# Prompt attention output through DRAM, layer norms placed between output-projection products, and lower step rates

## The chip, the core and the metric

The kernel runs on one core of a Trainium2 chip. The core has a matrix engine (PE in the profile, with PEld for its weight loads), a vector engine (DVE), an activation engine (ACT), a general engine (POOL) and a queue engine (SP) that here issues all DMAs. Each engine works its own instructions in a fixed order, and an instruction that waits holds up all behind it on that engine. On-chip memory is SBUF; matrix products land in eight PSUM banks of 128 x 512 floats. The metric is the device time of one execution in microseconds (us), lower is better.

## What is computed

Two batches, a prompt of 512 rows and a sample of 1024 rows, go through one encoder layer with shared weights (width 1024):

```
h = rmsnorm(x); z = h @ w_in                      # q | k | v | ca | cb
a = windowed attention(q, k, v), blocks of 128 rows, 8 heads, 2 kv groups
c = ca * sigmoid(cb); c = depthwise conv(31)(c); c = silu(layernorm(c))
x = x + concat(a, c) @ w_out
h = rmsnorm(x); u = depthwise conv(3)(h @ w_up)
x = x + (silu(gate) * value) @ w_down
y = rmsnorm(x)
```

All data is float32. A matrix product is done as three products of rounded parts (high x high, high x low, low x high), so every operand is first split in two by ACT (the high part) and POOL or DVE (the low part).

## The kernel before

**Order.** The program is written as one Python stream, and the place of an instruction in that stream is its priority. A planner then sets each engine's order: whenever an engine is free in its model of time, it takes the ready instruction of the best priority. On the chip this order is fixed. Slots in SBUF (`Slots`, 61 of 2 KB named h, 15 of 4 KB named q that can be halved, and a few others) and PSUM banks (a, u, b, c) are handed out in the order of the stream, so a new tile in a used slot waits for the last reader of the old one.

**Stages.** First, 14 column chunks of `w_in` are multiplied with the prompt (`step(i, 0)`). Then the same 14 chunks are loaded again and multiplied with both halves of the sample (28 products, `step(i, 1)` and `step(i, 2)`); beside these runs the prompt's own side work, the generator `prompt()`. Then follow 22 steps of the prompt's feed-forward part (`ffn_step`), beside which the sample's attention runs (`sample()`), then the sample's output projection and its feed-forward part.

**How side work is dosed.** A product of one chunk (`proj`) is 24 matmuls and calls `tick()` four times. A tick adds `pace["rate"]` to an account, and for every full unit one step (up to the next `yield`) of the front generator in `side` is put into the stream. The rates are `RB` beside the 28 products and `RBO` once the prompt's attention is through. What is left of `side` when the products are all in the stream is put behind them by `drain(side)`.

**The long convolution.** Each of 4 channel groups of a batch is a generator (`conv_items`): 27 (prompt) or 24 (sample) taps on DVE per 512 columns, one tap an item, and the other taps on ACT and POOL. `tick()` also gives credit for these items, at `CA` and then `CB` for the prompt's (`convs`), and, once these are through, at `CL`, `CLO` and `CD` in turn for the sample's (`late`). `behind` gives an item a priority that is `BACK` places later than its place in the stream.

**The prompt's side work before.** `attention(0, 8)` runs eight units (4 blocks of 128 rows, two kv groups each): `scores(u)` and `values(u)`. After each of units 4 to 7 one `conv_norm(i)` is run, for blocks 0 to 3; the first begins with `drain(convs)`, which puts all unfinished prompt convolution into the stream at that point. `values` leaves the attention's output of a block in two tiles `cats[i, 0]` (high and low part), and `conv_norm` the convolution's in `cats[i, 1]`. Then, for each half `n` of the output columns, the weights are loaded and split (`load_wo`, `split_wo`), and `out_half(i, n)` does 24 matmuls for each block (L726 to L728). The last half of a block adds the residual (L731), sums squares (L737) and computes the factor of the next norm. `make_h2` scales the four blocks (L776) and turns them (L258, with L260 and L261 taking the result to SBUF), which is the input of the feed-forward part.

**`conv_norm` step by step.** Load the block's convolution output (L684); four transposes into a bank (L690); mean and variance (L692, L693, on DVE); the factor (L176, L177, on POOL); scale (L696, DVE); four transposes back (L702); scale and bias (L705, four on ACT); tanh (L707); product (L708); high and low part (L709 on ACT, L710 on DVE).

The sample's attention output already goes through DRAM: `values` stores it to `catd` and `load_cat` fetches it.

Of the kernel before, what the change touches and what calls it, by code (L numbers as in the profile page):

```python
# [9 lines left out]
F32 = mybir.dt.float32  # L10
# [5 lines left out]
P = 128  # L16
D = 1024
KC = D // P
# [18 lines left out]

RA, RB, RBO, RD, RN, RE = 1.2, 0.8, 2.5, 0.8, 0.95, 0.9  # L40


CA, CB = 0.9, 0.4
CL, CLO, CD = 0.6, 1.0, 0.6

NOFF = (4, 7)

# [3 lines left out]
WOP, WOA, DW, DW2 = 1, 5, 2, 0  # L51
# [5 lines left out]
KEEP = 3  # L57


BACK = (200, 1500)  # L60
U0 = 2


# [82 lines left out]
def tile_hybrid_encoder(ctx: ExitStack, tc: tile.TileContext, xs, rel_bias, norm_attn_g, w_in,  # L146
                        attn_sink, conv_dw_w, conv_dw_b, conv_ln_g, conv_ln_b, w_out, norm_ffn_g,
                        w_up, ffn_dw_w, ffn_dw_b, w_down, norm_final_g, onehot, outs):
    nc = tc.nc
    cst = ctx.enter_context(tc.tile_pool(name="cst", bufs=1))  # L150
    big = ctx.enter_context(tc.tile_pool(name="big", bufs=1))
    dr = ctx.enter_context(tc.tile_pool(name="dr", bufs=1, space=bass.MemoryType.DRAM))
# [156 lines left out]
    qsd = [dr.tile([4, P, NH, P], F32, name=f"qsd{i}") for i in range(3)]  # L309
    vsd = dr.tile([P, 2, NKV, 4, P], F32, name="vsd")  # L310
    ksd = dr.tile([HD, NKV, 2, 1024], F32, name="ksd")
    catd = dr.tile([8, P, 2, 4 * P], F32, name="catd")
    cvd = [dr.tile([P, 4, G["T"]], F32, name=f"cvd{G['g']}") for G in GR]
    rs2 = cst.tile([P, 12], F32, name="rs2")

# [129 lines left out]
    def step(i, nt):  # L445
# [4 lines left out]
        if kind == "ca" and nt != 1:  # L450
            g = 0 if nt == 0 else 1
            (convs, late)[g].append(behind(conv_items(g, c, cpads.pop((g, c))), BACK[g]))
        tick()
# [76 lines left out]
    blocks = [(G, b) for G in GR for b in range(G["nb"])]  # L530
    NB = len(blocks)
    qt, cats, units = {}, {}, {}
# [86 lines left out]
    def values(u):  # L619
        i, kv = divmod(u, 2)  # L620
        G, b = blocks[i]
        kts = window(i)
        cat = cat_of(i, 0)
        pr = units.pop(u)
        nt0 = 0 if i < 4 else 1
        ht = []

        def turn(n):
            pt = bank("attn")
            for j in range(GRP):  # L630
                nc.tensor.transpose(pt[:, j * P:(j + 1) * P], pr[j][:, 1 + n * P:1 + (n + 1) * P], ident[:])
            hi, lo = sb.tile([NT], F32R), sb.tile([NT], F32R)
            nc.scalar.copy(hi[:], pt[:])
            nc.vector.tensor_tensor(lo[:], pt[:], hi[:].bitcast(F32), op=ALU.subtract)
            ht.append((hi, lo))

        turn(0)
        yield 0.0
        turn(1)
        po = bank("attn")  # L640
        for n, k in enumerate(kts):
            yield 0.0
            hi, lo = ht[n]
            v = vt[nt0 + k // 4][kv][:, k % 4, :]
            nc.tensor.matmul(po[:], v, hi[:], start=(n == 0), stop=False)
            nc.tensor.matmul(po[:], v, lo[:], start=False, stop=(n == len(kts) - 1))
            ht[n] = hi = lo = None
            if n + 2 < len(kts):
                turn(n + 2)
        rows = slice(kv * HD, (kv + 1) * HD)  # L650
        rest = slice((1 - kv) * HD, (2 - kv) * HD)
        c, d = sb.tile([NT]), sb.tile([NT])
        nc.scalar.copy(c[rows, :], po[rest, :])
        nc.scalar.copy(cat[0][rows, :, :], po[rows, :].rearrange("p (j t) -> p j t", t=P))
        nc.vector.tensor_tensor(d[rows, :], po[rows, :], cat[0][rows, :, :].bitcast(F32).rearrange("p j t -> p (j t)"),
                                op=ALU.subtract)
        nc.gpsimd.tensor_tensor(cat[1][rows, :, :].rearrange("p j t -> p (j t)"), d[rows, :], c[rows, :], op=ALU.add)
        if kv == 1 and G["g"] == 1:
            cats.pop((i, 0))
            for L in range(2):  # L660
                nc.sync.dma_start(catd[b, :, L, :].rearrange("p (j t) -> p j t", t=P), cat[L][:].bitcast(F32))
        yield 0.0

    def attention(u0, u1, then={}):
        yield from scores(u0)
        for u in range(u0, u1):
            if u + 1 < u1:
                yield from scores(u + 1)
            yield from values(u)
            if u in then:  # L670
                yield from then[u]

    def load_cat(i):
        cats[i, 0] = (sb.tile([4, P], F32R), sb.tile([4, P], F32R))
        for L in range(2):
            nc.sync.dma_start(cats[i, 0][L][:].bitcast(F32), catd[blocks[i][1], :, L, :].rearrange("p (j t) -> p j t", t=P))

    def conv_norm(i):
        G, b = blocks[i]
        if G["g"] == 0:  # L680
            drain(convs)
        cat = cat_of(i, 1)
        cv = sb.tile([4, P])
        nc.sync.dma_start(cv[:], cvd[G["g"]][:, :, b * P:(b + 1) * P])  # L684
        if G["g"] == 1 and (i, 0) not in cats:
            load_cat(i)
        yield 0.0
        pt = bank("norm")
        for c in range(4):
            nc.tensor.transpose(pt[:, c * P:(c + 1) * P], cv[:, c, :], ident[:])  # L690
        st, mv, rs = sm(6), sm(2), sm(1)
        nc.vector.bn_stats(st[:], pt[:])  # L692
        nc.vector.bn_aggr(mv[:], st[:])  # L693
        rstd_of(mv[:, 1:2], 1.0, rs[:])
        xh = sb.tile([CCH])
        nc.vector.tensor_scalar(xh[:], pt[:], mv[:, 0:1], rs[:], op0=ALU.subtract, op1=ALU.mult)  # L696
        del pt
        for _ in range(YN):
            yield 0.0
        p2 = bank("norm")  # L700
        for c in range(4):
            nc.tensor.transpose(p2[:, c * P:(c + 1) * P], xh[:, c * P:(c + 1) * P], ident[:])  # L702
        y, t = sb.tile([4, P]), sb.tile([4, P])
        for c in range(4):
            nc.scalar.activation(y[:, c, :], p2[:, c * P:(c + 1) * P], AF.Identity,  # L705
                                 scale=lng[:, c:c + 1], bias=lnb[:, c:c + 1])
        nc.scalar.activation(t[:], y[:], AF.Tanh)  # L707
        nc.vector.scalar_tensor_tensor(t[:], t[:], 1.0, y[:], op0=ALU.add, op1=ALU.mult)  # L708
        nc.scalar.copy(cat[0][:], t[:])  # L709
        nc.vector.tensor_tensor(cat[1][:], t[:], cat[0][:].bitcast(F32), op=ALU.subtract)  # L710
        yield 0.0

    xr, x1, wo = {}, {}, {}
    x1d = [dr.tile([P, D], F32, name=f"x1d{i}") for i in range(12)]

    def out_half(i, n):
        G, b = blocks[i]
        if i not in xr:
            xr[i] = load_x(G, b)
        x = xr[i]  # L720
        po = bank("out")
        s = slice(n * NT, (n + 1) * NT)
        for kc in range(KC):
            wh, wl = wo[kc, n]
            ch, cl = (t[:, kc % 4, :] for t in cats[i, kc // 4])
            nc.tensor.matmul(po[:], ch, wh[:], start=(kc == 0), stop=False)  # L726
            nc.tensor.matmul(po[:], ch, wl[:], start=False, stop=False)
            nc.tensor.matmul(po[:], cl, wh[:], start=False, stop=(kc == KC - 1))  # L728
            if kc % 2 == 1 and kc < KC - 1:
                yield 0.0  # L730
        nc.vector.tensor_tensor(x[:, s], po[:], x[:, s], op=ALU.add)  # L731
        if n == 1:
            x1[i] = x
            nc.sync.dma_start(x1d[i][:], x[:])
            ss = sm(1)
            junk = sb.tile([D], BF16, 2)
            nc.scalar.activation(junk[:], x[:], AF.Square, accum_out=ss[:])  # L737
            rstd_of(ss[:], D, rs2[:, i:i + 1])
            cats.pop((i, 0)), cats.pop((i, 1))
            xr.pop(i)  # L740
        yield 0.0
# [3 lines left out]
    def load_wo(kc, n):  # L745
        raw = wor[kc, n] = sb.tile([NT])
        s = slice(n * NT, (n + 1) * NT)
        if kc < 4:
            for kv in range(NKV):
                r0 = (kv * GRP + kc) * HD  # L750
                nc.sync.dma_start(raw[kv * HD:(kv + 1) * HD, :], w_out[0, r0:r0 + HD, s])
        else:
            nc.sync.dma_start(raw[:], w_out[0, kc * P:(kc + 1) * P, s])
# [28 lines left out]

    use.update(step="b", turn="a", attn="au", norm="au", out="u")

    def prompt():
        yield from attention(0, 8, {u: conv_norm(u - 4) for u in range(4, 8)})
        kt.clear(), vt.clear(), qt.clear(), bias.clear()
        pace.update(rate=RBO, late=CLO)
        for n in range(2):
            for kc in range(KC):  # L790
                if (kc, n) not in wor:
                    load_wo(kc, n)
            yield 0.0
            for kc in range(KC):
                split_wo(kc, n, kc % 2 < DW)
                if kc % 2 == 1:
                    yield 0.0
            for i in range(4):
                if n == 0 and i == 3:
                    for kc in range(WOP):  # L800
                        load_wo(kc, 1)
                yield from out_half(i, n)
            wo.clear()
        yield from make_h2(0, 0)

    seq = [(GR[0], j) for j in range(NJ)]
# [142 lines left out]
    L, R = slice(0, NT), slice(NT, W2)  # L949
# [634 lines left out]
    u, e, o11, o12 = (acc.pop(n) for n in ("u", "e", "o11", "o12"))  # L1584
# [73 lines left out]
```

## Time and profile before

| | |
|---|---|
| median of 3 runs | 1564.66 us (1561.09 to 1566.85) |
| the profiled execution | 1561.29 us |
| its span, first to last instruction | 1559.5 us |
| mean granted PE clock | 0.99 |
| PE busy | 1505.8 us, 97% of the span |
| DVE busy | 1126.9 us, 72% |
| ACT busy | 795.2 us, 51% |
| POOL busy | 709.7 us, 46% |
| DMA | 227.17 MB, mean 146 GB/s |

Times of places are in us from the first instruction. A row of the windows view gives a stretch, its length, then for each engine the busy time and the number of instructions, then the granted clock of PE (1.00 is full speed), the share of the DMA engines and GB/s. A row of the timeline gives the start, the length, engine, line, operation and, in square brackets, how long the engine had been idle and what ended that wait. `q<-a` is a write to a tile of class q from one of class a.

### The profile page before, as it was taken

How to read it: one execution, taken by the hardware profiler on the slowest of the kernel's cores; microseconds unless marked ns; L12 is line 12 of the kernel's file. 1: busy time of each engine (PE TensorE's matmuls, PEld its weight loads, DVE VectorE, ACT ScalarE, POOL GpSimd, SP SyncE). 2: the span in 40 equal slices, each digit the busy share in tenths (PEclk: the TensorE clock that was granted, in tenths of full speed). 3: DMA queues.
4: the chain of work that ended last, by engine and by line, in shares of the span. 5: the costliest groups of instructions: out<-in, count | busy, mean ns of one | idle time of the engine just before them, and what ended most of it. 6: DMA issues, size and time to landing. Idle time of an engine off the chain costs nothing. (4 is left out here: it accounts for less than half of the span.)

```text
span 1559.5 us, 20112 instructions
## 1 busy us (share of the span) xinstructions
PE 1505.8 (97%) x6843; PEld 1228.9 (79%) x6843; DVE 1126.9 (72%) x1604; ACT 795.2 (51%) x1404; POOL 709.7 (46%) x566
## 2 busy tenths in 40 slices
PE   8998998899999999899999999999999999999997
PEld 6787787787888888777777888888888788888885
DVE  7999767858789785334868777777776845569883
ACT  4634654335787786623455445554545543444354
POOL 6652343226666775947434555555544000003355
PEclk9999999899999999999999999999999999999999
DMA  7582334447344346779332333333332582357644
GB/s 229 157 212 78 108 99 124 128 131 226 111 132 130 117 130 182 241 235 305 108 95 75 102 101 102 102 102 102 102 115 75 191 280 82 105 166 233 220 132 162
DMA packets 228780, 227.17 MB, mean 146 GB/s; under 512 B 13268, under 2 KB 168348, under 8 KB 228549
## 3 DMA queue, kind: packets, MB, share of 16 engines
q1 hardware_dynamic: 228677, 225.88, 45.6%
q8 instruction: 54, 0.88, 0.2%
q14 instruction: 49, 0.40, 0.1%
HBM read 164.74 MB, written 62.14 MB: 145 GB/s over the span
## 5 line engine op out<-in xcount | busy, mean ns | idle before, releaser
L193 POOL TENSOR_TENSOR q<-q,q 128x1024 fp32r<-128x1024 f32 x72 | 173.3, 2414 | 93.5 <-ACT q L192 36.7
L955 POOL TENSOR_TENSOR q<-q,q 128x512 fp32r<-128x512 f32 x101 | 140.7, 1398 | 163.8 <-ACT q L1065 151.5
L955 DVE TENSOR_TENSOR h<-h,h 128x512 fp32r<-128x512 f32 (+2 forms) x202 | 158.4, 817 | 66.2 <-ACT h L959 26.1
L1413 PE MATMUL w<-h,h 128*128 128x512 f32 x462 | 181.4, 393 | 0.5 <-DVE q L1200 0.5
L1414 PE MATMUL w<-h,h 128*128 128x512 f32 x462 | 181.5, 393 | 0.0
L1415 PE MATMUL w<-h,h 128*128 128x512 f32 x462 | 181.1, 392 | 0.0
L1079 PE MATMUL w<-h,q 128*128 128x512 f32 x448 | 176.4, 394 | 3.0 <-ACT w L1171 1.6
L1081 PE MATMUL w<-h,q 128*128 128x512 f32 x448 | 175.5, 392 | 1.0 <-POOL q L955 1.0
L1080 PE MATMUL w<-h,q 128*128 128x512 f32 x426 | 166.5, 391 | 0.0
L299 PE MATMUL u<-h,q 128*128 128x512 f32 x400 | 161.1, 403 | 5.0 <-DVE h L852 4.2
L300 PE MATMUL u<-h,q 128*128 128x512 f32 x400 | 158.9, 398 | 0.0
L302 PE MATMUL u<-h,q 128*128 128x512 f32 x384 | 152.2, 396 | 2.7 <-POOL q L193 2.7
L952 POOL TENSOR_TENSOR q<-q,q 128x1024 f32<-128x1024 f32 x12 | 33.1, 2769 | 238.1 <-DMA h<-gb 197.4
L354 DVE SCALAR_TENSOR_TENSOR c<-c,cvw,c 128x512 f32<-128x512 f32 x184 | 137.9, 750 | 2.9
L959 ACT CAST h<-h 128x512 fp32r<-128x512 f32 x120 | 71.8, 619 | 95.9 <-DVE h L955 42.5
L299 PE MATMUL b<-h,q 128*128 128x512 f32 x256 | 102.3, 400 | 2.7 <-DVE d L384 1.9
L1413 PEld LDWEIGHTS w<-h,h 128*128 128x128 f32 x462 | 86.8, 188 | 20.7 <-ACT h L959 0.9
L1415 PEld LDWEIGHTS w<-h,h 128*128 128x128 f32 x462 | 86.7, 188 | 19.7
L852 DVE SCALAR_TENSOR_TENSOR h<-u,fw,h 128x511 f32<-128x511 f32 x88 | 65.4, 744 | 50.8 <-ACT h L856 50.1
L1414 PEld LDWEIGHTS w<-h,h 128*128 128x128 f32 x462 | 86.8, 188 | 19.4
L1079 PEld LDWEIGHTS w<-h,q 128*128 128x128 f32 x448 | 84.2, 188 | 22.5 <-ACT w L1171 2.1
L302 PE MATMUL b<-h,q 128*128 128x512 f32 x256 | 101.3, 396 | 0.0
(417 smaller groups left out, 3680.3 us busy)
## 6 DMA issues: line engine op xcount, KB each, us to landing
q<-in_w_up SPq DMA_DIRECT2D x88, 512.0 KB
ga<-q SPq DMA_DIRECT2D x64, 256.0 KB
h<-ga SPq DMA_DIRECT2D x57, 256.0 KB
q<-in_w_in SPq DMA_DIRECT2D x28, 512.0 KB
h<-in_w_down SPq DMA_DIRECT2D x52, 256.0 KB
q<-in_x_sample SPq DMA_DIRECT2D x15, 512.0 KB
h<-qsd SPq DMA_DIRECT2D x24, 256.0 KB
x1d<-q SPq DMA_DIRECT2D x11, 512.0 KB
```

The lines of the kernel that those rows point to most:

```text
L193: (nc.vector if dve else nc.gpsimd).tensor_tensor(lo[:], raw[:], hi[:].bitcast(F32), op=ALU.subtract)
L299: nc.tensor.matmul(out, whi[:, kc, :], hi[:], start=(kc == 0), stop=False)
L300: nc.tensor.matmul(out, whi[:, kc, :], lo[:], start=False, stop=False)
L302: nc.tensor.matmul(out, wlo[:, kc, :], hi[:], start=False, stop=(kc == KC - 1))
L354: nc.vector.scalar_tensor_tensor(acc[:], src(t), w(t), acc[:], op0=ALU.mult, op1=ALU.add)
L955: (eng or nc.vector).tensor_tensor(out, a, b, op=ALU.subtract)
L1079: nc.tensor.matmul(out, whi[:, s], hi[:], start=(start and c == 0), stop=False, **go)
L1080: nc.tensor.matmul(out, whi[:, s], lo[:], start=False, stop=False, **go)
L1081: nc.tensor.matmul(out, wlo[:, s], hi[:], start=False, stop=(stop and c == 3), **go)
L1413: nc.tensor.matmul(out, sh[:, c], th[:], start=(p == 0), stop=False)
L1414: nc.tensor.matmul(out, sh[:, c], tl[:], start=False, stop=False)
L1415: nc.tensor.matmul(out, sl[:, c], th[:], start=False, stop=(p == NPAIR - 1))
```

## The change

```diff
-RA, RB, RBO, RD, RN, RE = 1.2, 0.8, 2.5, 0.8, 0.95, 0.9
-CA, CB = 0.9, 0.4
-CL, CLO, CD = 0.6, 1.0, 0.6
+RA, RB, RBO, RD, RN, RE = 1.2, 0.7, 0.6, 0.8, 0.95, 0.9
+CA, CB = 0.85, 0.4
+CL, CLO, CD = 0.55, 0.9, 0.66
...
-BACK = (200, 1500)
+BACK = (200, 600)
...
-    catd = dr.tile([8, P, 2, 4 * P], F32, name="catd")
+    catd = dr.tile([12, P, 2, 4 * P], F32, name="catd")
...
-        if kv == 1 and G["g"] == 1:
+        if kv == 1:
             cats.pop((i, 0))
             for L in range(2):
-                nc.sync.dma_start(catd[b, :, L, :]..., cat[L][:].bitcast(F32))
+                nc.sync.dma_start(catd[i, :, L, :]..., cat[L][:].bitcast(F32))
...
-        if G["g"] == 1 and (i, 0) not in cats:
+        if (i, 0) not in cats:
             load_cat(i)
...
-        if n == 1:
+        halves_done[i] = halves_done.get(i, 0) + 1
+        if halves_done[i] == 2:
             x1[i] = x
...
+    def beside(gen, other):
+        for _ in gen:
+            yield 0.0
+            if next(other, None) is not None:
+                yield 0.0
+        yield from other
+
     def prompt():
-        yield from attention(0, 8, {u: conv_norm(u - 4) for u in range(4, 8)})
+        yield from attention(0, 8)
         kt.clear(), vt.clear(), qt.clear(), bias.clear()
         pace.update(rate=RBO, late=CLO)
-        for n in range(2):
+
+        def w_half(n):
...
-            for i in range(4):
-                if n == 0 and i == 3:
-                    for kc in range(WOP):
-                        load_wo(kc, 1)
+
+        for i in range(2):
+            yield from conv_norm(i)
+        yield from w_half(0)
+        yield from out_half(0, 0)
+        yield from beside(out_half(1, 0), w_half(1))
+        for i, n in ((0, 1), (1, 1)):
+            yield from beside(out_half(i, n), conv_norm(i + 2))
+        for n in (1, 0):
+            for i in (2, 3):
                 yield from out_half(i, n)
-            wo.clear()
+            for kc in range(KC):
+                wo.pop((kc, n))
         yield from make_h2(0, 0)
```

The prompt's attention output is stored to DRAM, block by block, and loaded back when a block's `conv_norm` begins. All attention units now come before the first `conv_norm`. Blocks 0 and 1 are normed first; the weights of the first column half are split; block 0 and block 1 are multiplied by them, the second half's weights being split beside block 1; the second halves of blocks 0 and 1 alternate in the stream with the norms of blocks 2 and 3; at the end come the second and then the first halves of blocks 2 and 3, and `make_h2`. The squares of a block are summed once both of its halves are done, in whatever order. The body of `w_half` is the old loop that loads and splits one half's weights. Fewer side steps are put into the stream per tick (`RB`, `RBO`), and the convolution's credit per tick is lower beside the first products (`CA`) and for the sample's part beside the 28 products (`CL`, `CLO`), and higher in the prompt's feed-forward part (`CD`); the sample's convolution items stand 600 instead of 1500 places behind.

More of the change, by code (lines that the diff above doesn't have):

```diff
@@ L657, in values @@
         nc.gpsimd.tensor_tensor(cat[1][rows, :, :].rearrange("p j t -> p (j t)"), d[rows, :], c[rows, :], op=ALU.add)
-        if kv == 1 and G["g"] == 1:
+        if kv == 1:
             cats.pop((i, 0))
             for L in range(2):
-                nc.sync.dma_start(catd[b, :, L, :].rearrange("p (j t) -> p j t", t=P), cat[L][:].bitcast(F32))
+                nc.sync.dma_start(catd[i, :, L, :].rearrange("p (j t) -> p j t", t=P), cat[L][:].bitcast(F32))
         yield 0.0
@@ L675, in load_cat @@
         for L in range(2):
-            nc.sync.dma_start(cats[i, 0][L][:].bitcast(F32), catd[blocks[i][1], :, L, :].rearrange("p (j t) -> p j t", t=P))
+            nc.sync.dma_start(cats[i, 0][L][:].bitcast(F32), catd[i, :, L, :].rearrange("p (j t) -> p j t", t=P))
     def conv_norm(i):
@@ L711, in conv_norm @@
         yield 0.0
-    xr, x1, wo = {}, {}, {}
+    xr, x1, wo, halves_done = {}, {}, {}, {}
     x1d = [dr.tile([P, D], F32, name=f"x1d{i}") for i in range(12)]
```

## The prediction

> **What bounds the kernel now.** First the page's busy times, then the windows view, to find where the matrix engine is not busy.
>
> ```profile
> PE 1505.8 (97%) x6843; PEld 1228.9 (79%) x6843; DVE 1126.9 (72%) x1604; ACT 795.2 (51%) x1404; POOL 709.7 (46%) x566
> ...
> 150.00:175.00 25.00, 20.46 (x98) 15.52 (x97) 22.66 (x50) 18.59 (x44) 8.97 (x7) 0.93 0.37 102
> ...
> 250.00:275.00 25.00, 18.88 (x89) 14.88 (x87) 15.76 (x26) 11.53 (x21) 15.01 (x12) 0.96 0.42 112
> 275.00:300.00 25.00, 22.29 (x88) 17.88 (x89) 19.52 (x28) 12.09 (x23) 7.09 (x6) 0.84 0.56 174
> ```
>
> PE is the bound and the change takes no matmul from it, so it can only win back idle time and slow clock. PE is idle for 1559.5 - 1505.8 = 53.7 us in all; in the stage that the change rearranges it is 4.5 us at 150 to 175 and 6.1 + 2.7 us at 250 to 300, where the clock falls to 0.84. Next the timeline there, and the windows view of the hole alone.
>
> ```profile
> 267.44 0.39 PE L302 MATMUL b<-h,q 128*128 128x512 f32 x1
> ...
> 268.35 0.72 ACT L346 ACTIVATE q<-c,cvw 128x512 f32<-128x512 f32 x1 [4.89 <-PE a L690]
> ...
> 270.83 0.57 POOL L177 TENSOR_TENSOR s<-s,nhalf 128x1 f32<-128x1 f32 x1
> ...
> 271.43 0.81 DVE L696 TENSOR_SCALAR q<-a,s,s 128x512 f32<-128x512 f32 x1 [2.21 <-POOL s L177]
> 272.30 0.66 PE L702 MATMUL u<-ident,q 128*128 128x128 f32 x4 [4.03 <-DVE q L696]
> ...
> 276.75 1.08 PE L702 MATMUL u<-ident,h 128*128 128x128 f32 x4 [2.97 <-DVE h L696]
> ...
> 281.07 0.60 ACT L388 ACTIVATE h<-b 128x512 fp32r<-128x512 f32 x1
> ...
> 283.17 0.39 PE L299 MATMUL b<-h,q 128*128 128x512 f32 x1
> 283.40 0.40 PE L300 MATMUL b<-h,q 128*128 128x512 f32 x1
> ```
>
> ```profile
> 268.30:283.20 14.90, 6.97 (x23) 5.28 (x24) 7.43 (x13) 9.32 (x19) 7.81 (x9) 0.66 0.38 121
> ```
>
> The norms of blocks 2 and 3 stand on PE with nothing between their transposes: PE waits 4.03 us and then 2.97 us for the statistics to pass through DVE and POOL. No projection fills in, because the last one (267.44) still sits in its bank: its evacuation L388 stands on ACT behind the norm's own steps, until 281.07. ACT had itself been held 4.89 us by a convolution tap (L346) whose tile took the slot that the norm's transposes were reading: SBUF slots are short. In these 14.9 us PE issued 23 instructions; at the 0.23 us from 283.17 to 283.40 (a transpose takes less) they need at most 5.3 us. **The hole costs at least 9.6 us**, about 10.
>
> **The change, part by part.** The sum is made against the profiled execution's 1561.29 us, its span of 1559.5 and 1.8 around it. The median of the runs is 3.4 us above it, so the result is moved up by that.
>
> *1. Norms spread out, output in DRAM.* Eight tiles (four blocks, high and low) no longer lie in h slots from the attention to the products. Norms 0 and 1 come after all units, one step per 1/0.6 tick, that is per 10 matmuls or 2.3 us, with projections between; norms 2 and 3 alternate with second-half products, of which two give 48 x 0.23 = 11 us of cover against single waits of 4.03 and 2.97. Bounds: -10 (hole gone) to 0 (it moves). I take -10, since cover and slots both improve. A further gain is the attention's own stretch at 150 to 175 (4.5 us idle): the side rate falls by an eighth, and DVE, 22.66 of 25 us there, gets that much less. Bounds -4.5 to +2 (a unit's chain could also come late), I take -3.
>
> *2. The added DMAs.* Eight stores and eight loads of 256 KB; SP is charged as for the sample's:
>
> ```profile
> L661 SPq DMA_DIRECT2D catd<-h x16: 319/320/532, 431.5 to 651.6; - x16
> L676 SPq DMA_DIRECT2D h<-catd x16: 319/386/430, 639.1 to 748.6; - x16
> ```
>
> 8 x 0.32 + 8 x 0.39 = 5.7 us of SP, over some 200 us. A store waits on SP for the low part (POOL L657); queued behind it are query stores and loads and weight loads, which are issued well ahead. I cost it at nothing, hidden by the 28 products; at the worst all 5.7 us are late for a weight chunk. The loads that bear on PE are those of blocks 2 and 3, a rival below.
>
> *3. The handover to the feed-forward part.* Steps to `prompt()`: attention is 52 (two per `scores`, nk + 2 per `values` with nk = 2, 3, 3, 2). Before: 68 with the norms, at 0.8, is tick 85 of the 112 that 28 products have; the other 50 (10 of weights, 32 of products, 8 of `make_h2`) at 2.5 end at tick 105. After: 52 at 0.7 is tick 74; norms 8, weights 5, first product 4 at 0.6 end near tick 103, and tick 112 falls in block 1's first product. Six halves and `make_h2` then stand behind the last projection. What projections covered before is this chain after the last output product:
>
> ```profile
> 353.42 0.39 PE L728 MATMUL u<-h,h 128*128 128x512 f32 x1
> ...
> 353.85 0.69 DVE L731 TENSOR_TENSOR q<-u,q 128x512 f32<-128x512 f32 x1 [0.83 <-PE u L728]
> ...
> 354.57 1.06 ACT L737 ACTIVATE h<-q 128x1024 bf16<-128x1024 f32 x1 [1.52 <-DVE q L731]
> ...
> 356.08 0.55 POOL L177 TENSOR_TENSOR rs<-rs,nhalf 128x1 f32<-128x1 f32 x1
> ...
> 356.69 0.75 DVE L776 TENSOR_SCALAR q<-q,rs 128x1024 f32<-128x1024 f32 x1
> ...
> 366.03 0.62 PE L299 MATMUL u<-h,q 128*128 128x512 f32 x2
> 366.49 0.60 PE L258 MATMUL a<-ident,q 128*128 128x128 f32 x4
> ```
>
> ```profile
> L299 PE MATMUL b<-h,q 128*128 128x512 f32 x16 | 6.5, 404 | 0.0
> ```
>
> ```profile
> L260 ACT ACTIVATE h<-a,vecs x8: 670/680/689, 364.7 to 372.0; 128x512 fp32r<-128x512 f32 x8
> L261 DVE SCALAR_TENSOR_TENSOR h<-a,vecs,h x8: 739/743/752, 365.4 to 372.9; 128x512 fp32r<-128x512 f32 x8
> ```
>
> From 353.81 to 357.44 the block is added, squared and scaled: 3.6 us. Four transposes 0.6, L260 0.68 and L261 0.74 follow, with hops between them 6.0 us to the first feed-forward matmul. Before, 16 x 3 projection matmuls (the count between 353.6 and 366) filled it, 11 us of work; now nothing of the prompt does. What can fill in are the first scores of the sample, which before already ran here:
>
> ```profile
> 372.98 0.39 PE L575 MATMUL a<-q,h 128*128 128x256 f32 x2
> ```
>
> They need only queries, keys and bias from DRAM. Bounds: +2 (scores fill 4 us) to +11 (a POOL split of 2.4 us is ahead of L177, 8.4 in all, and the clock drops). I take +4: two units' scores, 16 matmuls of at most 0.2 us, some 2 us, come in.
>
> The clock after a hole is the part that no single row settles.
>
> ```profile
> 155.00:160.00 5.00, 4.22 (x13) 2.63 (x12) 4.94 (x10) 3.16 (x8) 2.07 (x2) 0.68 0.81 212
> ...
> 275.00:280.00 5.00, 2.29 (x7) 1.72 (x8) 3.36 (x5) 2.71 (x6) 0.69 (x3) 0.50 0.67 217
> ```
>
> ```profile
> PE u L631 <- DVE s L582: 2.0, 2, 1.1
> PE a L645 <- ACT h L633: 1.2, 1, 1.2
> ```
>
> After the waits of 4.03 and 2.97 the clock was 0.50, so a hole of 6 us would cost slow matmuls too. The Trainium skill (TensorE: Matmul & The Clock Gate, section Part 1: The HAM clock gate) speaks against the change here: an idle window of about 3.4 us halves the clock, and it stays so for as long again. By that rule a handover of 6 us would cost about 1.7 us more, an estimate from that page, and one of under 3.4 us nothing. The first half agrees with the 0.50 above; the second does not, since at 155 to 160 the clock was 0.68 where no wait was over 1.2 us.
>
> *4. The convolution's pace.* Credit for the prompt's items lasts to about tick 74 instead of 39, without the burst of `drain`; the sample's gets 37 x 0.9 = 33 instead of 46 x 0.6 + 27 x 1.0 = 55. An item costs 0.663, so about 32 of them move into the feed-forward part.
>
> ```profile
> L354 DVE SCALAR_TENSOR_TENSOR c<-c,cvw,c x106: 717/748/756, 349.9 to 576.7; 128x512 f32<-128x512 f32 x106
> ```
>
> ```profile
> 350.00:625.00 275.00, 273.50 (x1327) 228.56 (x1326) 218.72 (x424) 200.61 (x378) 180.04 (x112) 1.00 0.48 148
> ...
> 450.00:475.00 25.00, 25.00 (x124) 20.97 (x123) 23.32 (x44) 18.53 (x36) 18.81 (x12) 1.00 0.46 147
> ...
> 625.00:650.00 25.00, 25.00 (x118) 20.56 (x118) 9.56 (x14) 19.42 (x33) 24.92 (x18) 1.00 0.83 266
> ```
>
> 32 x 0.748 = 24 us on DVE, which has 275 - 218.7 = 56 us free there and runs at 23.32 of 25 in its fullest stretch with PE at 25.00. The items end near 617 instead of 577, since 99 credits at 0.66 are 151 of the 176 ticks. PE hides it: bounds 0 to +5, I take +0.5.
>
> **Sum**: -10 - 3 + 4 + 0.5 = -8.5 on 1561.3, that is 1552.8; on the median's footing 1564.7 - 8.5 = **1556 us**.
>
> **Rivals.** *A, the handover opens fully:* no scores come in, because the keys' q slots are freed only by `make_h2`. +8.4, the clock +1.7, and -1 instead of -3 in the attention: -10 - 1 + 10 + 0.5 = -0.5, 1564 us. For it: the keys were fetched at the pace at which blocks were scaled, the last two after block 3's product. Against: 32 h slots fall free with the last projection.
>
> ```profile
> 349.90 1.09 SPq L763 DMA_DIRECT2D q<-ksd  x2
> ...
> 354.02 1.10 SPq L763 DMA_DIRECT2D q<-ksd  x2
> ```
>
> *B, slower: the hole moves behind the last projection.* Tiles of norms 2 and 3 take slots that the last projection reads, so their loads start only then. A load of 512 KB was seen to take 6 us:
>
> ```profile
> 352.92 0.38 SPq L186 DMA_DIRECT2D q<-in_w_up  x1
> ...
> 359.12 1.05 ACT L192 CAST q<-q 128x1024 fp32r<-128x1024 f32 x1 [3.40 <-DMA q<-in_w_up]
> ```
>
> With 6 us of load, some 3.5 of statistics and 4.5 of L705 to L710, block 2 is ready after 14 us. Cover is the rest of block 1's first half (1.4), two second halves (11) and the first half of block 2's (2.8): 15.2. It decides once the queues of SP, ACT and POOL add over 1.2 us. If both norms come late as they did at 268, PE loses 9 us there and 10 at the handover: -10 + 19 = +9, 1574 us. Against it: the planner can bring other products forward.
>
> *C, the pace does not do what it says:* items that end near 617 push splits of the sample's weights into 625 to 650, where POOL has 24.92 of 25; PE then waits there for 5 us. -8.5 + 5 = -3.5, 1561 us.
>
> **How the numbers follow.** Forecast 0.45, A 0.2, B 0.25, C 0.1. About 0.5% (8 us) is what a measurement can tell from no change. The forecast lies at that bound on the faster side; nearly all its chance and a little of C is faster, A and most of C the same, B and a little of A slower: 0.5, 0.22, 0.28. Range: the forecast with all lower bounds is -10 - 4.5 + 2 = -12.5, and earlier queue relief may add some, 1546; upwards it takes in B, 1574. The forecast's own is 1550 to 1561.
>
> **What would show it.** Right: no wait at L702 over 2 us before the feed-forward part, PE near 25.00 where the norms are, and a PE gap of 2 to 5 us between the last L728 and the first feed-forward L299, with L575 in it. A: a gap of 8 us and a clock near 0.5 behind it. B: waits at L690 or L702 between output products, put down to loads or DVE. C: full PE up to 600 and more idle time behind 650. It would be wrong altogether if the time came from beyond the sample's output projection, whose code is untouched.

## The result and the profile after

| | median | range | runs |
|---|---|---|---|
| before | 1561.52 us | 1557.86 to 1566.85 | 20 |
| after | 1565.82 us | 1562.68 to 1572.18 | 20 |

The ratio is 1.0026 with a 95% interval of 1.0016 to 1.0036: 0.26% slower, about 4 us. The forecast was 8.5 us faster, and 1556 us because it started from the first three runs of before, whose median is 3 us above that of all 20. The profiled execution took 1568.68 us, its span 1566.9 us, 7.4 more than the span of before; some 3 us of that is this execution's own, which lies above its median.

First the page's busy times and the windows view of after, at the stretches shown of before and two that are new.

```profile
PE 1512.0 (96%) x6843; PEld 1231.9 (79%) x6843; DVE 1132.6 (72%) x1604; ACT 795.9 (51%) x1404; POOL 712.8 (45%) x566
...
150.00:175.00 25.00, 22.78 (x98) 17.90 (x97) 21.73 (x42) 14.48 (x31) 8.86 (x6) 0.86 0.45 137
...
250.00:275.00 25.00, 25.00 (x119) 20.59 (x118) 13.17 (x17) 13.37 (x26) 13.90 (x13) 1.00 0.73 208
275.00:300.00 25.00, 24.44 (x107) 19.73 (x106) 22.84 (x33) 10.01 (x17) 9.03 (x7) 1.00 0.38 124
...
350.00:375.00 25.00, 18.79 (x86) 14.62 (x86) 18.14 (x25) 9.52 (x15) 10.98 (x10) 0.86 0.40 130
375.00:400.00 25.00, 20.64 (x89) 16.80 (x88) 18.32 (x43) 13.36 (x26) 10.67 (x7) 0.93 0.36 103
```

The hole at the norms is gone: PE is idle 0.6 us between 250 and 300 instead of 8.8, at full clock. In its place PE is idle 6.2 us at 350 to 375 and 4.4 us at 375 to 400, with the clock at 0.86 and 0.93. The timelines of PE, then POOL, DVE, SP and ACT, show how both come about.

```profile
353.75 0.40 PE L728 MATMUL u<-h,h 128*128 128x512 f32 x1
355.21 0.55 PE L258 MATMUL a<-ident,q 128*128 128x128 f32 x3 [1.06 <-DVE q L777]
360.55 0.90 PE L258 MATMUL a<-ident,q 128*128 128x128 f32 x3 [4.79 <-DVE q L777]
361.81 1.22 PE L299 MATMUL u<-h,q 128*128 128x512 f32 x2 [0.35 <-ACT h L260]
...
373.99 0.40 PE L575 MATMUL a<-q,h 128*128 128x256 f32 x2
...
377.26 0.40 PE L575 MATMUL a<-q,h 128*128 128x256 f32 x2
382.02 0.62 PE L299 MATMUL u<-h,q 128*128 128x512 f32 x1 [4.36 <-DVE h L869]
```

```profile
355.24 2.35 POOL L193 TENSOR_TENSOR q<-q,q 128x1024 fp32r<-128x1024 f32 x1 [0.63 <-DVE q L777]
357.54 1.26 POOL L347 TENSOR_TENSOR h<-h,h 128x512 f32<-128x512 f32 x1
358.89 0.19 POOL L176 TENSOR_SCALAR rs<-s 128x1 f32<-128x1 f32 x1
```

```profile
355.08 0.68 DVE L731 TENSOR_TENSOR q<-u,q 128x512 f32<-128x512 f32 x1
...
359.74 0.75 DVE L777 TENSOR_SCALAR q<-q,rs 128x1024 f32<-128x1024 f32 x1 [0.21 <-POOL rs L177]
```

```profile
360.57 12.17 SPq L186 DMA_DIRECT2D q<-in_w_up  x3
```

```profile
375.71 1.05 ACT L192 CAST q<-q 128x1024 fp32r<-128x1024 f32 x1 [2.44 <-DMA q<-in_w_up]
377.39 1.04 ACT L192 CAST q<-q 128x1024 fp32r<-128x1024 f32 x1 [0.64 <-DMA q<-in_w_up]
378.35 1.44 ACT L873 ACTIVATE h<-u,vecs,fw 128x512 f32<-128x512 f32 x2
```

After the last output product (353.75) PE has three transposes of the block before (355.21) and then nothing until the block that this product finishes has been added, squared and scaled. It is added at 355.08, squared by 356.9, and then its factor (L176) stands on POOL behind a weight split of 2.35 us and a convolution sum of 1.26 us until 358.89. The first feed-forward matmul starts 7.7 us after the last product's end.

The second gap, 4.36 us before 382.02, begins with late weight chunks of `w_up`. The first was fetched at 360.57 and the next only at 371.74, because SP waited for the slots that PE's last transposes were reading:

```profile
SPq L186 <- PE a L258: 10.8, 1, 10.8
```

ACT's splits of these chunks (L192) waited for them, and behind the splits stands the step L873 that reads the bank which PE needs next; DVE's L869 reads it last. So the second gap follows from the first: the scaled blocks keep their slots until PE has turned them.

To compare kernels I add up what PE loses in each 25 us stretch: 25 less the busy time, plus the busy time times (1 - granted clock). The stage bounds are the same for all, so a kernel that is late blurs them a little.

| us lost on PE | 100 to 250 | 250 to 350 | 350 to 425 | 650 to 850 | ratio to before |
|---|---|---|---|---|---|
| before | 9.0 | 13.2 | 1.5 | 13.8 | 1 |
| after | 10.2 | 0.6 | 14.7 | 15.7 | 1.0026 |
| after, again | 10.2 | 0.6 | 14.7 | 18.5 | 1.0034 |
| e5_null | 10.4 | 13.6 | 2.0 | 14.3 | 1.0003 |
| e2_new_rates | 8.7 | 12.3 | 15.4 | 17.4 | 1.0079 |
| e4_old_conv | 11.6 | 10.6 | 15.2 | 19.4 | 1.0104 |
| e7_conv | 14.3 | 1.1 | 8.9 | 15.1 | 1.0008 |
| x1_dram | 26.2 | 11.2 | 5.7 | 17.8 | 1.0156 |
| v1_norms | 7.9 | 13.3 | 1.5 | 17.1 | 1.0025 |
| e6_no_wait | 8.9 | 2.7 | 4.3 | 16.8 | 0.9983 |
| v2_scores4 | 9.9 | 2.3 | 13.1 | 25.9 | 1.0096 |
| v3_held | 8.4 | 0.1 | 18.6 | 15.2 | 1.0031 |
| v3_held_fast | 10.7 | 0.0 | 10.7 | 16.8 | 0.9990 |
| v4_pin2 | 9.4 | 8.2 | 0.8 | 8.3 | 0.9934 |
| v4_pin1 | 10.5 | 10.8 | 10.7 | 16.9 | 1.0074 |

By this account the change won 12.6 us at the norms and paid 13.2 us at the handover, so these two nearly cancel. By the same account the time by which it is slower lies in the other stages, which lose 5.9 us more than in the one profile of before, and 6.5 us more in the second profile of after: some 1 us in each profile at 100 to 250, 1.9 and 4.7 us at 650 to 850, the rest ahead of 100 and behind 850. What makes these is not shown; part of it is the clock, which differs from one execution to the next (last section).

### The profile page after: what moved, and what is told of

Same layout as the page of the kernel before. It is cut to its first block, busy times and chain, and to the rows that moved or that the text cites. A ratio compares the mean times of both kernels' runs of the same rounds, so it can differ in the third digit from the quotient of the medians.

```text
span 1566.9 us, 20161 instructions
## 1 busy us (share of the span) xinstructions
PE 1512.0 (96%) x6843; PEld 1231.9 (79%) x6843; DVE 1132.6 (72%) x1604; ACT 795.9 (51%) x1404; POOL 712.8 (45%) x566
## 5 line engine op out<-in xcount | busy, mean ns | idle before, releaser
L299 PE MATMUL u<-h,q 128*128 128x512 f32 x400 | 162.1, 407 | 6.5 <-DVE h L869 4.4
L299 PE MATMUL b<-h,q 128*128 128x512 f32 x256 | 103.0, 402 | 3.5 <-DVE d L384 2.9
L192 ACT CAST q<-q 128x1024 fp32r<-128x1024 f32 x72 | 75.5, 1050 | 58.9 <-DMA q<-in_w_in 28.0
L1431 PEld LDWEIGHTS w<-h,h 128*128 128x128 f32 x462 | 86.8, 188 | 19.4
```

Of the source, the lines that this page charges most:

```text
L299: nc.tensor.matmul(out, whi[:, kc, :], hi[:], start=(kc == 0), stop=False)
L1431: nc.tensor.matmul(out, sh[:, c], tl[:], start=False, stop=False)
```

## Experiments

**Which part makes what.** The first two runs take one group of edits back, the next two apply one part alone.

e2_new_rates, the code of before with all constants of after:

```diff
-RA, RB, RBO, RD, RN, RE = 1.2, 0.8, 2.5, 0.8, 0.95, 0.9
+RA, RB, RBO, RD, RN, RE = 1.2, 0.7, 0.6, 0.8, 0.95, 0.9
-CA, CB = 0.9, 0.4
-CL, CLO, CD = 0.6, 1.0, 0.6
+CA, CB = 0.85, 0.4
+CL, CLO, CD = 0.55, 0.9, 0.66
-BACK = (200, 1500)
+BACK = (200, 600)
```

> Order and storage of before, with all the new rates of the change. Theory (the change removes a hole of some 12 us at the norms by its order, and opens one of some 13 us at the handover because six products stand behind the last projection): 68 steps at 0.7 are 97 ticks, then 9 of the other 50 steps fit, so the handover opens here as well: PE idle of 5 to 11 us between the last L728 and the feed-forward part, and 8 to 13 us slower than before (about 1572), unless the norms' hole goes too (then about 1561). Rival (the convolution's pace is what costs): 4 us slower, with no gap at the handover.

Measured: 1577.61 us, ratio 1.0079 (1.0061 to 1.0097). PE's longest waits between 100 and 900:

```profile
PE a L258 <- DVE q L776: 7.3, 1, 7.3
PE u L726 <- ACT h L192: 5.7, 1, 5.7
PE u L299 <- DVE h L852: 4.0, 1, 4.0
```

The theory held, with a loss of 13 us: the handover opens in the old order as well (L258 waits 7.3 us for the scaling), once the rate leaves products for after the last projection. The rival expected no gap there. The norms' hole is replaced by another in the same stage: the first product waits 5.7 us for the splits of its weights.

e4_old_conv, after with the old convolution pace:

```diff
-CA, CB = 0.85, 0.4
-CL, CLO, CD = 0.55, 0.9, 0.66
+CA, CB = 0.9, 0.4
+CL, CLO, CD = 0.6, 1.0, 0.6
-BACK = (200, 600)
+BACK = (200, 1500)
```

> The changed kernel with the convolution's old pace (CA, CL, CLO, CD, BACK of before), RB and RBO new. Theory: the same gap at the handover, time within 3 us of the changed kernel (1563 to 1569). Rival (the pace costs): back to about 1561, by the rows behind 375 us.

Measured: 1580.09 us, ratio 1.0104 (1.0079 to 1.0129). Neither expectation held.

```profile
328.09 1.11 PE L690 MATMUL a<-ident,h 128*128 128x128 f32 x4 [5.78 <-DMA h<-cvd]
```

This is PE's timeline. With the old pace the new order loses 10.6 us at 250 to 350 instead of 0.6, above all at the norm of block 3, which waits for its load. The lower pace is not what costs; with the new order it gains.

x1_dram, before with the attention output through DRAM alone (the edits of the diff at `catd`, `values`, `conv_norm` and `load_cat`):

> Before with one part alone: the prompt's attention output stored to DRAM and loaded back at the block's norm; order and rates of before. Theory (order makes the hole): within 3 us of before, the hole at 268 still there. Rival (short slots make the hole): the hole shrinks by 5 us or more and the time with it, 1551 to 1556.

Measured: 1588.63 us, ratio 1.0156 (1.0133 to 1.0179). Neither expectation held. The storage alone is a loss of 24 us: 17 us of it in 100 to 250. PE's window at 225 to 250, where before had 0.2 us idle, and the longest waits between 225 and 425:

```profile
225.00:250.00 25.00, 17.62 (x66) 13.28 (x67) 13.03 (x28) 11.25 (x27) 4.04 (x4) 0.73 0.40 98
```

```profile
PE a L702 <- DVE h L696: 4.5, 1, 4.5
PE u L299 <- ACT h L260: 3.5, 1, 3.5
```

At the norms PE now waits over 2 us once, 4.5 us at block 0, instead of 4.03 and 2.97 us at blocks 2 and 3, so the hole at 268 is gone, which the rival expected of free slots. But the time is lost elsewhere: attention units, which still alternate with the norms in this order, wait for steps on ACT and DVE and for queries (up to 2.1 us each, at L575, L631 and L645), and the clock is 0.73 in the window above. Whether short slots made the hole, this run does not decide.

v1_norms, before with norms 2 and 3 between the first-half products of blocks 0 and 1 (`beside` is that of the change):

```diff
-        yield from attention(0, 8, {u: conv_norm(u - 4) for u in range(4, 8)})
+        yield from attention(0, 8, {u: conv_norm(u - 4) for u in range(4, 6)})
...
-                yield from out_half(i, n)
+                if n == 0 and i < 2:
+                    yield from beside(out_half(i, n), conv_norm(i + 2))
+                else:
+                    yield from out_half(i, n)
```

> Before with one part alone: norms of blocks 2 and 3 alternate with the first-half products of blocks 0 and 1; output stays in SBUF, old order of the weight halves, old rates, so that projections still stand behind the last product. Theory: no waits over 2 us at the norms, handover covered, 8 to 12 us faster than before (1549 to 1553). Rival (a new plan only moves the holes): 1558 to 1564.

Measured: 1568.28 us, ratio 1.0025 (1.0011 to 1.0039). The waits at the norms are gone, the loss of the stage is not:

```profile
PE b L299 <- DVE q L389: 3.7, 2, 2.5
PE b L299 <- ACT q L375: 3.4, 2, 2.1
```

Now the projections wait for their banks, which ACT and DVE empty late. The rival held in kind, though the time is 4 us above its range: the hole moved.

**Is any new plan a loss?** e5_null, the smallest change that makes the planner plan anew:

```diff
-CL, CLO, CD = 0.6, 1.0, 0.6
+CL, CLO, CD = 0.6, 1.0, 0.62
```

> Before with the sample's convolution pace in the prompt's feed-forward part at 0.62 instead of 0.6 and nothing else: as small a change as can be made that plans the program anew. Theory (each part has its own cost): within 2 us of before. Rival (before sits in a good plan and any new one loses several us in places that were not touched): 3 to 10 us slower, in stretches behind 400 us.

Measured: 1564.80 against 1564.02 us, ratio 1.0003 (0.9991 to 1.0015). This new plan was no loss, as the theory had it.

e7_conv, before with the new convolution pace alone (the last three constants of e2_new_rates):

> Before with the convolution's new pace alone (CA, CL, CLO, CD, BACK of the change), order, storage and step rates of before. Theory (the new order removes the norms' hole): the hole at 250 to 300 stays, time within 3 us of before. Rival (the lower pace removes it, since with the old pace the new order had a wait of 5.8 us for a norm's load): 5 to 12 us faster than before.

Measured: 1565.18 us, ratio 1.0008 (0.9995 to 1.0021). The hole at 250 to 300 is gone, by pace alone, as the rival had it; the time is not better, as windows of this kernel show:

```profile
225.00:250.00 25.00, 20.09 (x86) 16.00 (x87) 24.56 (x46) 14.43 (x34) 6.57 (x6) 0.86 0.47 127
250.00:275.00 25.00, 25.00 (x117) 20.46 (x116) 17.16 (x28) 12.92 (x24) 12.46 (x9) 1.00 0.69 172
...
350.00:375.00 25.00, 22.76 (x107) 17.97 (x106) 19.54 (x29) 12.03 (x19) 13.12 (x10) 0.93 0.83 255
```

It loses 7.7 us at 225 to 250, where DVE is full and PE waits 3.7 us for the load of block 1's norm (L690), so part of the hole has moved ahead. It also loses 8.9 at the handover, though the step rates are those of before: with products for cover behind the last output product, the first feed-forward matmul waits 1.6 us for L260, but the second kind of gap is there (L299 waits 3.5 us for L852). Over 100 to 350 together the losses are 22.2 us in before, 15.3 here and 10.8 in after; e2_new_rates, e4_old_conv and v1_norms stay at 21 to 22.

**What the handover costs.** e6_no_wait, after with the feed-forward input loaded instead of made:

```diff
-            a = sb.tile([D])
-            nc.vector.tensor_scalar_mul(a[:], x1[k][:], rs2[:, k:k + 1])
+            a = load_x(GR[g], i)
             x1.pop(k)
             ts.append(a)
```

> The changed kernel, with the prompt's feed-forward input loaded from the prompt itself instead of scaled from the output projection: left out are the prompt's residual sum and norm in that place, so that nothing there waits for the last product. Theory (the chain from the last product to the first feed-forward product costs 6 us of idle time and 2 to 4 us of slow clock): the gap at 355 to 362 is gone and the kernel is 6 to 10 us faster than the changed one (1556 to 1560). Rival (the feed-forward part starts badly for other reasons, splits and taps): the gap moves to its first steps, under 3 us gained.

Measured: ratio to before 0.9983 (0.9972 to 0.9994), against 1.0026 of after, so 0.43% or 6.7 us better than after, as the theory had it. The handover loses 4.3 instead of 14.7 us, the second gap having gone as well; 4.9 us are lost at 625 to 650, where after lost 0.1.

v2_scores4, after with the sample's first scores ahead of `make_h2`:

```diff
-        yield from make_h2(0, 0)
...
+    units_left = attention(8, 24)
+    for _ in range(4):
+        next(units_left)
+    for _ in make_h2(0, 0):
+        pass
...
-        yield from attention(8, 24)
+        yield from units_left
```

> The changed kernel, with the scores of the sample's first two units put into the program ahead of the prompt's last scaling and turning, so that they can run in the gap of the handover; same work in all. Theory: 2 to 4 us of matmuls and transposes move into the gap, the gap falls from 6 to 2 to 4 us, the time by 2 to 5 us (1561 to 1564). Rival (keys and queries come too late to fill it): no gain, within 2 us of the changed kernel.

Measured: 1576.62 us, ratio 1.0096 (1.0068 to 1.0123). The 16 score matmuls ran between 338 and 346, ahead of the gap, and L258 still waits 5.5 us; the stretch at 650 to 850 lost 10 us more. Neither expectation held. Keys and queries were there in time, but an earlier place in the program did not put the scores into the gap.

**Cover given back.** v3_held puts the last two chunks' products with the sample's second half into the program behind the last output product, beside `make_h2`, with the same work:

```diff
-        yield from make_h2(0, 0)
...
-    for i in range(npr, nch):
+    for i in range(npr, nch - 2):
...
+    want_w(nch - 1)
+    for i in (nch - 2, nch - 1):
+        step(i, 1)
+    h1.pop(1)
+    drain(side)
+    side.append(make_h2(0, 0))
+    for i in (nch - 2, nch - 1):
...
+        step(i, 2)
```

> The changed kernel with cover given back: the products of the last two weight chunks with the sample's second half (48 matmuls, 11 us) are put into the program behind the prompt's last output product, beside make_h2. All work is the same. Theory (the handover costs some 13 us because nothing covers the chain): the gap at 355 to 382 falls under 3 us, the norms stay without a hole, and the kernel is 8 to 13 us faster than the changed one, 0.3 to 0.6% faster than before. Rival (a plan moves its holes): the handover is covered, but as much is lost elsewhere, within 3 us of the changed kernel.

v3_held_fast adds `pace.update(rate=2.0)` behind `side.append(make_h2(0, 0))`.

> The same, with make_h2 put into the program at 2 steps a tick instead of 0.6, so that its transposes stand ahead of most of the held products. Theory: the same or 1 to 2 us better than v3_held, as the feed-forward input is ready earlier. Rival: as there.

> The changed kernel as it is, on the same chip as the two above, for a second profile: the gap behind the last L728 and the low clock after it should be there again (10 us idle and 3 to 4 us of slow clock in 350 to 425), being fixed by the order; the low clock at 50 to 75 and 100 to 125, with the same idle time as before, should differ from profile to profile.

Measured, on one chip: v3_held 1.0031 (1.0021 to 1.0041), v3_held_fast 0.9990 (0.9976 to 1.0004), after again 1.0034 (1.0021 to 1.0047). Neither expectation of v3_held held: the handover loses 18.6 us and the kernel is no faster than after. v3_held_fast is 5.6 us better than v3_held, more than expected. The gaps of after came back to the tenth of a microsecond, in idle time and in slow clock; the low clock at 50 to 75 and 100 to 125, which was expected to differ, came back as well (last section). The held products did not stand in the gap: in v3_held_fast only 7 of the 48 matmuls ran behind the last output product, since they were ready and the planner used them up before. PE's longest waits of v3_held_fast between 225 and 425:

```profile
PE a L258 <- DVE q L777: 4.6, 1, 4.6
PE u L299 <- ACT h L260: 2.8, 1, 2.8
```

v4_pin2 is v3_held_fast with the held products tied on PE behind the last output matmul:

```diff
-            nc.tensor.matmul(po[:], cl, wh[:], start=False, stop=(kc == KC - 1))
+            last = nc.tensor.matmul(po[:], cl, wh[:], start=False, stop=(kc == KC - 1))
...
+        ends.append(last.ins)
...
-        step(i, 2)
+        with tc.issue_after(ends[7]):
+            step(i, 2)
```

> v3_held_fast, with both held products tied on PE behind the last output product, so that 48 matmuls (11 us) do stand in the gap: in v3_held_fast all but 7 of the held matmuls had run before it. All work is the same. Theory (the gap is there for want of cover alone): idle time in 350 to 425 falls from 10.6 us to under 3 and slow clock from 4.1 to under 1, and the kernel is 6 to 12 us faster than the changed one, ratio to before 0.995 to 0.999. Rival (what is won there is lost in the stages behind, whose plan is new each time): the gap closes and the ratio to before is 1.000 or more.

v4_pin1 does so with the last product alone.

> The same with the last product alone held back and tied (24 matmuls, 5.5 us against a chain of 6). Theory: idle time in 350 to 425 of 1 to 4 us, clock nearly full, ratio to before 0.996 to 1.000. Rival: as in v4_pin2.

Measured: **v4_pin2 1553.58 us against 1564.38, ratio 0.9934 (0.9911 to 0.9957)**; v4_pin1 1576.08 us, ratio 1.0074 (1.0056 to 1.0092). Windows of v4_pin2, then PE's longest waits of it between 225 and 425 and of v4_pin1 between 100 and 900:

```profile
325.00:350.00 25.00, 20.59 (x82) 16.09 (x81) 16.90 (x25) 5.82 (x11) 3.09 (x4) 0.93 0.49 126
350.00:375.00 25.00, 24.95 (x126) 19.70 (x125) 21.22 (x29) 12.81 (x19) 12.59 (x10) 1.00 0.69 209
```

```profile
PE u L728 <- DMA h<-catd: 2.7, 1, 2.7
PE u L726 <- DMA h<-catd: 1.7, 1, 1.7
```

```profile
PE u L299 <- DVE h L878: 7.9, 3, 4.6
...
PE a L258 <- DVE q L778: 2.0, 1, 2.0
```

With 48 matmuls in the gap the handover loses 0.8 us, and this kernel is faster than before and than after, as the theory had it. The gap at the handover is there for want of cover. The ratio is 0.92% better than that of after, 14 us, but this sum has more parts: by the table 13.9 us come from the handover, 7.6 are lost again at 250 to 350 (products waiting for the attention output from DRAM among them), and 7.4 are won at 650 to 850, where no code was changed. Without that stretch the gain would be some 7 us, inside the range of the theory; the rest is luck. With 24 matmuls, 5.5 us, L258 still waits 2.0 us, and the stage before it and the first feed-forward steps have holes again: half a cover did not pay, against both expectations.

## Why the prediction was wrong, step by step

*Bound.* Right in that the change takes no matmul away and the large moves are idle time and clock of PE in the prompt's stage. Not seen: the stages outside it lose some 5 us more as well.

*Step 1, the norms (-10).* Right in effect, by 12.6 us with the clock. The reason was only half right. I credited order and free slots; x1_dram shows that the storage alone costs, v1_norms that a like order of the norms with the old pace only moves the hole, e7_conv that the pace alone removes it from that place, with part of it back at 225 to 250, and e4_old_conv that the new order without the pace keeps a loss of 10.6 us. Over 100 to 350 together, only kernels with the new order, the storage and the new pace come near half the loss of before; whether the storage is needed is open, since no run has order and pace without it. The further 3 us at 150 to 175 did not come: 2.3 us less idle time, 1.8 us more slow clock.

*Step 2, the DMAs at nothing.* Not hidden everywhere: the storage cost 24 us in the old order (x1_dram), and in v4_pin2 products wait 4.4 us for these loads. After itself shows no such wait before 400.

*Step 3, the handover (+4)*, **is the step that failed.** The count of steps and ticks and the missing projections were as worked out: the gap lies between the last L728 and the first feed-forward L299. The chain itself is 7.7 us against my 6.0. Its factor waits 2.0 us in POOL's queue, which is the case of my upper bound; its sum waits 0.9 us on DVE behind the scaling of the block before; and from the scaling to the first matmul it is 1.1 us shorter than I had it. The +4 falls short of the measured +13.2 in three places. The first gap is 6.2 us of idle time, 2.2 us more, since no score ran in it. The clock behind the two gaps takes 4.1 us, for which +4 had nothing. And the second gap takes 4.4 us, against 1.5 us of idle time at 375 to 400 in before; I had no term for it at all. So the scores, on which I chose the value, are only the smallest of the three.

Why no score filled the gap can be read from the trace. I wrote that the scores need only queries, keys and bias from DRAM. SP's timeline of after shows that these were fetched ahead of the gap, the keys at 310 to 319 and the first queries at 350, the biases in between:

```profile
309.94 2.94 SPq L764 DMA_DIRECT2D q<-ksd  x4
...
316.85 2.38 SPq L764 DMA_DIRECT2D q<-ksd  x4
...
350.01 1.94 SPq L539 DMA_DIRECT2D h<-qsd  x3
```

But a score also needs a PSUM bank. The first three write class a, which has three banks, and in the program they stand behind `make_h2`, whose transposes use these banks. Three groups were turned as far as the last block but one (L258 x3 at 355.21) and held one bank each until that block's last three transposes at 360.55 and the steps behind them. By the order in which banks are handed out, the first score gets the bank of the sixth of the eight groups, whose transposes ran at 367.56; it ran at 373.99, 20 us after the last output product. This is a reading of the trace and the program: no run gave the scores other banks in the same place.

*Step 4, the pace (+0.5).* The items did end later, but far fewer moved than I had counted:

```profile
L354 DVE SCALAR_TENSOR_TENSOR c<-c,cvw,c x115: 718/749/757, 361.3 to 605.6; 128x512 f32<-128x512 f32 x115
```

These are the items of after behind 350 us, ending at 606 against my 617, and 115 against 106, only 9 more instead of 32. PE hid them: 0.1 us lost at 425 to 650. That the pace matters most for the stage before, I had not seen.

*The sum.* Taken over the whole kernel, the account of the table puts the profile of after 6.5 us above that of before, where -8.5 was forecast. Of these 15 us, 9.2 are the handover, 4.2 the stretch at 100 to 250 (-3 forecast, +1.2 measured) and 4.7 the stages that had no term; the norms, 2.6 us better than forecast, and the pace, 0.4 better, go against them.

*The rivals.* A was nearest: the handover opens with a clock of 0.50 behind it, no score comes in, the norms' gain is given back, 1564 us. Its reason was not what happened, since the keys' slots did not wait for `make_h2`, and it had neither the second gap nor the losses outside the prompt's stage; that its time comes so near is in part luck. I gave it 0.2 because I took one coincidence, scores that ran in the gaps of the first feed-forward steps, for a rule. B did not occur in after, but in e4_old_conv (a norm waits 5.8 us for its load) and, smaller, in v4_pin2. C's wait at 650 was there in before already (7.1 us lost at 650 to 675) and is 8.7 in after: a small part.

*The clock rule.* That a gap of this size costs clock too, as the Trainium skill has it (TensorE: Matmul & The Clock Gate, section Part 1: The HAM clock gate), agreed. The estimate from that page, 1.7 us for a gap of 6 us, which rival A had as its term for the clock, was too low for the first gap: its slice lost 2.6 us, and that of the second gap 1.4 us. The granted clock was 0.50 from 359 to 365, some 3 us beyond the start of the first feed-forward matmul.

## What to carry to other kernels

When side work is moved later, count what the matrix engine still has to do beside the last dependent chain: a chain that was free under other products costs its full length, its queue waits, the slow clock after it, and whatever its slots hold up behind it. When a product is counted on to fill a gap, look for everything it needs, its output bank included. A place in the program is no place on an engine where a planner fills gaps greedily; cover that is wanted at one point has to be tied there. And a part whose removal empties a hole is no gain until the total shows it, since several of these kernels emptied or moved the same hole and were no faster.

## What the runs showed of the hardware

The clock falls late and comes back late. Two windows of after, 1 us each, in and behind the first gap:

```profile
357.00:358.00 1.00, 0.00 (x0) 0.00 (x0) 0.00 (x0) 0.00 (x0) 1.00 (x2) 1.00 0.87 352
...
364.00:365.00 1.00, 1.00 (x4) 0.71 (x4) 1.00 (x2) 0.61 (x1) 0.00 (x0) 0.50 0.00 0
```

PE had nothing to do from 355.8, the clock was still at 1.00 up to 358, and it was at 0.50 at 364 to 365, when PE was busy all the time again.

Idle time summed over a window does not tell the clock. Windows of before, of after and of after again:

```profile
50.00:75.00 25.00, 21.13 (x107) 16.60 (x106) 24.82 (x36) 17.11 (x26) 18.09 (x15) 1.00 0.40 110
```

```profile
50.00:75.00 25.00, 21.30 (x103) 16.87 (x102) 24.27 (x35) 16.22 (x25) 19.31 (x16) 0.93 0.41 113
```

```profile
50.00:75.00 25.00, 21.99 (x104) 17.56 (x105) 24.61 (x36) 16.90 (x26) 18.14 (x15) 0.93 0.41 112
...
150.00:175.00 25.00, 21.91 (x98) 17.17 (x97) 21.34 (x41) 14.30 (x30) 8.59 (x5) 0.93 0.47 137
```

At 50 to 75, 3.9 us idle left the clock at 1.00 in before, while 3.7 and 3.0 us brought it to 0.93 in both profiles of after. The longest single wait there was 1.9 us in before and 2.9 us in both profiles of after, so here the clock goes with the longest wait. At 150 to 175 it does not: after had 0.86 with 2.2 us idle in one execution and 0.93 with 3.1 us in the other, which is 3.2 and 1.5 us of slow clock for the same program. Over the 20 runs of after the mean clock goes from 0.985 in the slowest (1572.18 us) to 0.991 in one of 1564.06 us: much of what one run differs from the next is clock, so stages of single profiles are compared to some 2 us, not better.

A load can be held up by a store that has nothing to do with its data. SP's timeline of after at the sample's first output product, then SP's and PE's waits there:

```profile
651.97 0.36 SPq L900 DMA_DIRECT2D gt<-h  x1
...
657.16 0.33 SPq L676 DMA_DIRECT2D h<-catd  x1
```

```profile
SPq L676 <- DMA gt<-h: 3.4, 1, 3.4
```

```profile
PE c L726 <- DMA h<-catd: 5.1, 1, 5.1
```

By the program, the block of this load had been stored to `catd` long before, among the stores at 430 to 467. What the load waited for is put down to the store of the feed-forward part issued at 651.97, whose h slot it can take over only when that store has read it. The load was issued at 657.16 and the product that needs it started at 660.38, after a wait of PE of 5.1 us. In the second profile of after the same two waits are 3.7 and 4.8 us.
